# A two-layer convolution and pooling trunk: one address phase for all operands of the products, and one task for the feed-forward modulation

## The chip, the cores and the metric

The kernel runs on one core of one Trainium2 chip. The metric is the device time of one execution in microseconds (us); of several executions the median is given. A profile is one further execution, recorded instruction by instruction, with a time of its own.

The engines are named as in the profile: PE (TensorE, the products), PEld (its weight loads), DVE (VectorE), ACT (ScalarE), POOL (GpSimd), SP (SyncE, which only issues transfers). In the trace the instructions of an engine stand in the order in which the program holds them.

## The reference

The input is one sequence of 1024 positions with 1024 channels, and one conditioning vector `c`. There are two layers. In each, a modulated RMS norm feeds a token mixer (layer 0: a causal convolution module, layer 1: a causal pooling mixer), a second modulated norm feeds a gated feed-forward part, and both results are added back with a gate:

```python
c_act = jax.nn.silu(c)
for i in range(DEPTH):
    mod = c_act @ ada_w[i] + ada_b[i]
    sh_m, sc_m, g_m, sh_f, sc_f, g_f = jnp.split(mod, N_ADA, axis=-1)
    h = modulate(rms_norm(x, norm_mix_g[i]), sh_m, sc_m)
    y = conformer_conv(h, ...) if i % N_MIXERS == 0 else multiscale_pool(h, ...)
    x = x + (1.0 + g_m)[:, None, :] * y
    h = modulate(rms_norm(x, norm_ffn_g[i]), sh_f, sc_f)
    y = swiglu_ffn(h, ...)          # (silu(h @ w_gate) * (h @ w_up)) @ w_down, inner width 2816
    x = x + (1.0 + g_f)[:, None, :] * y
return rms_norm(x, final_g)
```

`conformer_conv` is a product 1024 to 2048 with a gated linear unit, a causal depthwise convolution of width 31, a layer norm over channels, silu, and a product 1024 to 1024. Everything is float32.

## The kernel before

**Layout.** Channels lie on the 128 partitions in 8 tiles (`KT`), positions along the free dimension in two chunks of 512, A and B. A chunk passes through a whole stage before the other does: the convolution part of A, then of B, and the feed-forward part of A and of B, in both layers.

**Products.** To keep float32 accuracy, both factors are split into a high and a low part. `products` (L423) issues three matmuls for each weight block of 128 x 128: weight-high by activation-high, weight-high by activation-low, weight-low by activation-high. The activations are the moving operands, 512 columns of 4 bytes; their pairs are called `hhi`/`hlo` (normed input), `vhi`/`vlo` (convolution output), `ghi`/`glo` (inside the feed-forward part), `mxhi`/`mxlo` (pooling) and `uhi`/`ulo` (the part of the depthwise convolution that is done on PE with diagonal weights). The results go to `first`, `a`, `g` (first product of the convolution module), `y` (its last product), `gate`, `up` and `dn` (feed-forward).

**Tiles of the activations.** `slot` (L239) takes one of 16 buffers for each chunk. Chunk B's are 512 floats wide. Chunk A's are 514 floats wide (`slot_after`, L243), with two columns ahead for the shifted reads of the taps on PE, and A's operands begin at the third float. `wslot` (L247) gives tiles of 542 floats (512 and a halo of 30 ahead), 8 for each chunk; `u` (convolution input), `hp` (pooling input) and `ghi`/`glo` share them. In the built program the allocator rounds the pitch of these tiles up to a multiple of 32 or 64 bytes, so the moving operands begin at these addresses modulo 256 bytes: chunk B's `hhi`, `hlo`, `vhi`, `vlo` all at 64; chunk A's at 8, 40, 72, 104, 136, 168, 200 or 232, from tile to tile; `ghi`, `glo` of both chunks at 64 or 192. All weights begin at 64.

**Taps.** The depthwise convolution of each channel tile is a `Taps` task (L666) of 31 taps, most of them `SCALAR_TENSOR_TENSOR` on DVE (`ca`), some on POOL (`pa`). For A's tile 7 all 31 taps, and for tile 6 eight of them, are done on PE (`pe_taps`, L636). `split_u` (L628) makes `uhi`/`ulo` of tile 6, `conv_glu` (L583) those of tile 7.

**Modulation.** `c_act @ ada_w` is done as dots on DVE: for 128 outputs a tile `adaw` of 128 x 1024 floats (512 KB) is loaded, multiplied by `cact` and summed (`ada_dot`, L315); 8 dots make one of the six vectors of a layer. `ada_task` (L324) does them with a pause between dots, with two buffers: a load is issued when the dot before last is done. For layer 0's feed-forward part there are two such tasks (L1144), vector 5 (gate) and vector 4 (scale), begun when the layer norm of A has been written out, ahead of A's last convolution product.

**What sets the order.** The program is written once as a list of units in PE's order. After every few products `pace` (L187) lets waiting tasks put instructions on DVE and POOL, by clocks that the planner estimates. The constants in `LOAD` are pauses of that clock. `finish` (L199) puts out all that is left of a task. Weights are loaded up to 5 ahead (`W_BUFS`): SP loads the raw tile (`raw`), ACT makes the high part and the negative of it, and a transfer of POOL's queue adds the raw tile to make the low part. SP's queue is one for `raw` and `adaw`.

**Around the change.** The order of PE there is: taps of A on PE, two tiles of B's first product, the mean of A's layer norm (`mean`), A's last product `y` in 8 output tiles with the sum of squares of the next norm behind each, one tile of B's first product (`a`, `g`) into which that norm is laid (`var`, then `rstd`), and then the first unit of the feed-forward part. All stand on DVE in the program's order with the dots.

Of the kernel before, what the change touches and what calls it, by code (L numbers as in the profile page):

```python
# [9 lines left out]
F32 = mybir.dt.float32  # L10
# [6 lines left out]
P = 128  # L17
# [9 lines left out]
PHALO = max(WINDOWS) - 1  # L27
EPS = 1e-6
# [20 lines left out]
LOAD = {"load": 4.0, "slow": 18.0, "next": 4.0, "dots": 3.5}  # L49
# [65 lines left out]
def trunk(ctx, tc, xT, c, vec, ada, adan, w1f, w1, wdg, w2, wgu, wdn, wpl, out):  # L115
# [208 lines left out]
    def ada_task(l, js, pause=None):  # L324

        def gen():
            todo = [(j, k) for j in js for k in range(KT)]
            ws = [ada_load(ada[(l * 6 + j) * KT + k]) for j, k in todo[:ADA_BUFS]]
            for i, (j, k) in enumerate(todo):
                yield pause or ("next" if lax[0] else "slow")  # L330
# [244 lines left out]
    def conv_u(ch, p):  # L575
        u = st["u", ch.i, p] = wslot(ch, "u")
# [6 lines left out]
    def conv_glu(ch, p, ba, bg):  # L583
# [3 lines left out]
        if ch.i == 0 and PE_TAPS.get(p) == CW:  # L587

            V_.scalar_tensor_tensor(ba, ba, V("conv_b1", p), sg, op0=ADD, op1=MUL)
            hi, lo = st["us", p] = [slot_after(A, name) for name in ("uhi", "ulo")]  # L590
            for part in (hi, lo):
                G_.memset(part[:, :2].bitcast(F32), 0.0)
            S_.copy(hi[:, 2:], ba)
            V_.tensor_tensor(lo[:, 2:], ba, hi[:, 2:].bitcast(F32), op=SUB)
# [6 lines left out]
    def conv_in(*todo):  # L601

        def emit(take):
            got = {}
            for each in todo:
# [30 lines left out]
    def pe_taps(p):  # L636

        groups = tap_groups(p)
        us = []
        for i, js in enumerate(groups):  # L640
            def emit(take, i=i, js=js):
# [18 lines left out]
    class Taps:  # L660
# [599 lines left out]
```

## Time and profile before

| | |
|---|---|
| runs | 1871.35, 1873.54, 1875.83 us; median 1873.54 |
| profiled execution | 1871.14 us, of which the span from first to last instruction is 1869.4 us |
| busy share of the span | PE 98%, PEld 79%, DVE 53%, ACT 52%, POOL 33% |
| mean granted clock of PE | 0.993 |
| transfers | 387.56 MB, 207 GB/s over the span |
| chain that ended last | PE 82%, DVE 10%, DMA 6%, the rest 2% |

A busy PE is not a PE at its peak: matmuls overlap, and the mean duration of one (393 ns for 512 columns) is longer than the distance from one start to the next. That distance has to be read from the starts, in the timeline of PE. Rows of the timeline give the start in us from the span's start, the time until the end of the last of the merged instructions in us, and in square brackets how long the engine stood idle before, and what ended that.

### The profile page before, as it was taken

Reading aid. Unit: us, or ns where it says so; the run is one execution under the profiler, and the core shown is the slowest. Engines: PE = TensorE matmul, PEld = TensorE weight load, DVE = VectorE, ACT = ScalarE, POOL = GpSimd, SP = SyncE. Lnnn points to the kernel's source line nnn. Section 1 sums busy time; section 2 is a strip of 40 time slices with the busy share of each in tenths; the row PEclk is TensorE's granted clock in tenths of the full one; section 3 lists DMA queues with packets and bytes.
Section 4 is the critical chain, followed back from the end, with each engine's and each line's share of the span. In section 5 each row is a group of like instructions: output and inputs, shape, how many; then the busy total and the mean of one; then the engine's idle time right before and its main releaser. Section 6 shows DMA issues by size and latency. Waiting matters only on the chain.

```text
span 1869.4 us, 21783 instructions
## 1 busy us (share of the span) xinstructions
PE 1826.0 (98%) x8085; PEld 1481.9 (79%) x8085; DVE 990.9 (53%) x1528; ACT 968.0 (52%) x1240; POOL 614.8 (33%) x662
## 2 busy tenths in 40 slices
PE   7999998999999999999999999999999999999997
PEld 5777776888888888877888888888888888888886
DVE  8899856988875235585622233734432233322225
ACT  3775665766656454454644445644534454444443
POOL 4587522877733211272111111511111111111111
PEclk9999998999999999999999999999999999999998
DMA  7958797888978987999887878778778879788782
GB/s 289 300 151 221 172 263 222 225 222 208 223 189 216 231 221 185 283 261 269 227 194 178 211 171 205 182 173 205 181 178 196 192 177 250 176 205 197 181 195 68
DMA packets 108285, 387.56 MB, mean 207 GB/s; under 512 B 11793, under 2 KB 13969, under 8 KB 108178
## 3 DMA queue, kind: packets, MB, share of 16 engines
q0 software_dynamic: 44208, 160.98, 47.2%
q1 hardware_dynamic: 62880, 224.13, 34.6%
q8 instruction: 64, 1.05, 0.2%
q10 hardware_dynamic: 1090, 1.05, 0.2%
q14 instruction: 43, 0.35, 0.1%
HBM read 381.92 MB, written 4.19 MB: 207 GB/s over the span
## 4 chain that ended last, share of the span: by engine, by line
PE 82%; DVE 10%; DMA 6%; issue 1%; ACT 1%; SPq 0%; POOL 0%; DVEq 0%
PE gate L131 24%; PE up L131 24%; PE dn L131 24%; DMA adaw<-in_ada_dram 5%; DVE ca L109 4%; PE y L131 4%; PE first L131 3%; DVE adaw L109 1%; DVE acc L109 1%; PE g L131 1%; PE a L131 1%; DVE x L109 1%; DVE t L109 1%; DMA adaw<-in_adan_dram 1%; DVE hlo L109 1%
## 5 line engine op out<-in xcount | busy, mean ns | idle before, releaser
L109 ACT CAST w<-raw 128x1024 fp32r<-128x1024 f32 x317 | 331.0, 1044 | 508.2 <-issue 303.8
L131 PE MATMUL gate<-hhi,w 128*128 128x512 f32 x1408 | 455.4, 393 | 2.3 <-DVE x L109 1.7
L131 PE MATMUL up<-hhi,w 128*128 128x512 f32 x1408 | 455.9, 393 | 0.0
L131 PE MATMUL dn<-ghi,w 128*128 128x512 f32 (+1 forms) x1440 | 445.7, 386 | 1.2 <-DMA w<-in_wdn_dram 1.2
L417 POOL DMA_DIRECT2D w<-in_wgu_dram x176 | 154.6, 878 | 779.0 <-ACT w L109 759.4
L109 ACT ACTIVATE w<-raw 128x1024 fp32r<-128x1024 f32 x307 | 323.9, 1055 | 0.0
L109 DVE SCALAR_TENSOR_TENSOR x<-dn,gains,x 128x512 f32<-128x512 f32 (+1 forms) x360 | 261.8, 735 | 115.8 <-PE dn L131 115.3
L109 DVE TENSOR_TENSOR t<-t,up 128x512 f32<-128x512 f32 x86 | 59.0, 686 | 495.0 <-PE up L131 474.8
L131 PEld LDWEIGHTS dn<-ghi,w 128*128 128x128 f32 x1440 | 267.9, 188 | 59.8 <-DMA w<-in_wdn_dram 1.6
L131 PEld LDWEIGHTS gate<-hhi,w 128*128 128x128 f32 x1408 | 264.8, 188 | 62.6 <-DVE x L109 2.5
L131 PEld LDWEIGHTS up<-hhi,w 128*128 128x128 f32 x1408 | 264.7, 188 | 59.2 <-DMA w<-in_wgu_dram 0.3
L131 PE MATMUL dn<-glo,w 128*128 128x512 f32 (+1 forms) x720 | 278.7, 387 | 0.0
L131 PE MATMUL gate<-hlo,w 128*128 128x512 f32 x704 | 276.7, 393 | 1.5 <-DVE hlo L109 1.5
L131 PE MATMUL up<-hlo,w 128*128 128x512 f32 x704 | 276.5, 393 | 0.0
L109 POOL TENSOR_TENSOR pa<-pa,pr 128x512 f32<-128x512 f32 x156 | 222.9, 1545 | 13.6 <-ACT pr L109 10.9
L109 DVE SCALAR_TENSOR_TENSOR ca<-u,vecs,ca 128x512 f32<-128x512 f32 x257 | 177.8, 745 | 0.5
L131 PEld LDWEIGHTS gate<-hlo,w 128*128 128x128 f32 x704 | 132.6, 188 | 31.5 <-DVE hlo L109 2.3
L131 PEld LDWEIGHTS dn<-glo,w 128*128 128x128 f32 x720 | 135.2, 188 | 28.1 <-issue 0.2
L131 PEld LDWEIGHTS up<-hlo,w 128*128 128x128 f32 x704 | 132.6, 188 | 29.2
L417 POOL DMA_DIRECT2D w<-in_wdn_dram x88 | 78.3, 890 | 228.4 <-ACT w L109 226.5
L109 DVE SCALAR_TENSOR_TENSOR adaw<-adaw,cact 128x1024 f32<-128x1024 f32 x80 | 118.9, 1488 | 65.1 <-DMA adaw<-in_ada_dram 65.0
L109 ACT ACTIVATE t<-gate 128x512 f32<-128x512 f32 x86 | 51.1, 594 | 157.4 <-PE gate L131 155.4
(145 smaller groups left out, 1776.7 us busy)
## 6 DMA issues: line engine op xcount, KB each, us to landing
raw<-in_wgu_dram SPq DMA_DIRECT2D x176, 512.0 KB, 7.5
w<-in_wgu_dram POOLq DMA_DIRECT2D x176, 512.0 KB, 8.1
raw<-in_wdn_dram SPq DMA_DIRECT2D x88, 512.0 KB, 5.3
w<-in_wdn_dram POOLq DMA_DIRECT2D x88, 512.0 KB, 9.4
adaw<-in_ada_dram SPq DMA_DIRECT2D x64, 512.0 KB, 7.6
raw<-in_w_dram SPq DMA_DIRECT2D x36, 512.0 KB, 6.4
w<-in_w_dram POOLq DMA_DIRECT2D x34, 512.0 KB, 8.5
adaw<-in_ada_dram SPq DMA_DIRECT2D x8, 1024.0 KB, 5.3
```

Of the source, the lines that this page charges most:

```text
L109: self.last = self.order(getattr(self.eng, name)(out, *args, **kw))
L131: last_mm[0] = nc.tensor.matmul(out, lhsT, rhs, start=start, stop=stop).ins.name
L417: order(nc.gpsimd.dma_start(low if len(src.shape) == 2 else low.rearrange("p (a b) -> p a b", a=src.shape[1]), src, accum_op=ADD))
```

## The change

Three things are changed.

**Addresses.** Chunk A's slots lose their two extra columns. The wide slots become pairs: one tile of 2 x 544 floats holds `u` (or `hp`) of two neighbouring channel tiles, or `ghi` at the front of the first half and `glo` at the end of the second (`gslots`); 4 pairs stand in for 8 singles. In the built program every moving operand of a product begins at 64 modulo 256 bytes, as the weights do, except the 93 taps of tile 7, which read shifted (at 52, 56, 180 and 184).

**Taps on PE.** Tile 6 has its eight taps on PE at even distances (j = 28, 26, ... 14), read from an unshifted copy, where it had the last eight; DVE and POOL do the other 23, the last of them in the task's end. Its split is made after A's last tile. The split of tile 7 lies in a pair of B's, with the halo columns cleared ahead of it.

**Modulation.** The two tasks of vectors 5 and 4 become one (`ada_f`), vector 4 first, whose first two loads are issued two tiles of B's first product earlier. Its first dot has the pause "slow" (18), the others "dots" (4.0, before 3.5). Behind A's last product only vector 4 is forced (`scale_done`); the rest runs on into the feed-forward part and is finished there after three units, and the task of layer 1 begins only then.

```diff
@@ tiles
     def slot(ch, name, dt=F32R):
-        return slot_after(ch, name, dt)[:, 2 - 2 * ch.i :]
-
-    def slot_after(ch, name, dt=F32R):
-        return slots.tile([P, ch.n + 2 - 2 * ch.i], dt, tag=f"s{ch.i}", name=nm(name))
-
-    def wslot(ch, name, dt=F32):
-        return slots.tile([P, ch.width], dt, tag=f"u{ch.i}", name=nm(name), bufs=KT)
+        return slots.tile([P, ch.n], dt, tag=f"s{ch.i}", name=nm(name))
+
+    def wpair(ch, name, dt=F32):
+        return slots.tile([P, 2, WSLOT], dt, tag=f"u{ch.i}", name=nm(name), bufs=KT // 2)
+
+    def wslot(ch, name, p):
+        if st.get((name, "pair", ch.i), (None,))[0] != p // 2:
+            st[name, "pair", ch.i] = p // 2, wpair(ch, name)
+        return st[name, "pair", ch.i][1][:, p % 2, : ch.width]
+
+    def gslots(ch):
+        pair = wpair(ch, "g", F32R)
+        return pair[:, 0, : ch.n], pair[:, 1, WSLOT - ch.n :]
...
@@ ffn_p1
-            hi, lo = st["g", ch.i, f] = [wslot(ch, name, F32R)[:, : ch.n] for name in ("ghi", "glo")]
+            hi, lo = st["g", ch.i, f] = gslots(ch)
...
@@ tap_groups
-    todo = list(range(CW - 1, CW - 1 - PE_TAPS[p], -1))
+    n = PE_TAPS[p]
+    todo = list(range(CW - 1, -1, -1) if n == CW else range(CW - 3, CW - 3 - 2 * n, -2))
...
@@ Taps, end of the task
             d = u[:, HALO : HALO + n]
+            if self.part is not None:
+                V_.tensor_tensor(self.acc, self.part, self.acc, op=ADD)
+            V_.scalar_tensor_tensor(d, d, w(CW - 1), self.acc, op0=MUL, op1=ADD)
             if self.awaits:
-                if self.part is not None:
-                    V_.tensor_tensor(d, self.part, self.acc, op=ADD)
-                else:
-                    S_.copy(d, self.acc)
                 V_.tensor_tensor(d, d, self.other, op=ADD)
-            else:
-                if self.part is not None:
-                    V_.tensor_tensor(self.acc, self.part, self.acc, op=ADD)
-                V_.scalar_tensor_tensor(d, d, w(CW - 1), self.acc, op0=MUL, op1=ADD)
...
@@ the order of the units
     unit(lambda take: finish(*(T["taps", 0, p] for p in range(KT) if PE_TAPS.get(p, 0) < CW)))
+
+    unit(lambda take: T.__setitem__("ada_f", ada_task(0, (4, 5), "dots", "slow")))
     for p in rest[len(rest) - HOLD - HOLD_LN : len(rest) - HOLD]:
         conv_in((B, p))
     need("ln_a")
-
-    unit(lambda take: [T.__setitem__(("ada", 0, j), ada_task(0, (j,), "dots")) for j in (5, 4)])
     sq_a = Squares(A)
     conv_out(A, sq_a, lambda take: [now(columns_done(*g)) for g in held_back])
-    unit(lambda take: finish(T["ada", 0, 4]))
+    def scale_done(take):
+        forced[0] = True
+        while (0, 4) not in ada_done:
+            step(T["ada_f"], "V")
+        forced[0] = False
+    unit(scale_done)
...
-    unit(lambda take: T.__setitem__(("ada", 1), ada_task(1, range(6))))
     taps(B, *range(KT))
     put("ln_b", lambda: layer_norm_silu(B))
     fa = ffn(A, 0, False)
     for i, (e, ws) in enumerate(fa):
+        if i == GROUP + 1:
+            unit(lambda take: finish(T["ada_f"]))
+            unit(lambda take: T.__setitem__(("ada", 1), ada_task(1, range(6))))
```

PE's own order stays nearly as it was: apart from the taps, three short groups (a `mean`, a `var` and an `rstd`, of B's norms in layer 0) move by 6 to 24 products. What moves is on DVE and SP. In the rows a name's number is its buffer; all compute rows have the line of the recording helper, L109 before and L113 after.

DVE, from the last tile but one of `y` to the norm ahead of the feed-forward part of A (`x`: the residual update, `acc`: the sum of squares, `var` and `col`: its mean and reciprocal root, `t` and `hlo`: the normed input). Before, without rows of `var` and `col` that only repeat the chain:

```order
L109 SCALAR_TENSOR_TENSOR x_3_80<-t_2438,gains,x_3_80 128x512
L109 TENSOR_TENSOR acc_2221<-acc_2221,t_2441 128x512
L109 SCALAR_TENSOR_TENSOR adaw_2325,mod<-adaw_2325,cact 128x1024
L109 SCALAR_TENSOR_TENSOR x_3_80<-t_2477,gains,x_3_80 128x512
L109 SCALAR_TENSOR_TENSOR adaw_2365,mod<-adaw_2365,cact 128x1024
L109 TENSOR_TENSOR acc_2221<-acc_2221,t_2480 128x512
L109 SCALAR_TENSOR_TENSOR adaw_2368,mod<-adaw_2368,cact 128x1024
L109 TENSOR_SCALAR var_2540<-var_2540 128x4
L109 SCALAR_TENSOR_TENSOR adaw_2408,mod<-adaw_2408,cact 128x1024
L109 SCALAR_TENSOR_TENSOR col_2546<-var_2540,col_2546 128x4
L109 SCALAR_TENSOR_TENSOR adaw_2411,mod<-adaw_2411,cact 128x1024
L109 SCALAR_TENSOR_TENSOR t_2575<-x_0_77,gains,rstd_2570 128x512
```

And after the change:

```order
L113 SCALAR_TENSOR_TENSOR x_3_80<-t_2406,gains,x_3_80 128x512
L113 SCALAR_TENSOR_TENSOR adaw_2379,mod<-adaw_2379,cact 128x1024
L113 TENSOR_TENSOR acc_2201<-acc_2201,t_2409 128x512
L113 SCALAR_TENSOR_TENSOR x_3_80<-t_2446,gains,x_3_80 128x512
L113 TENSOR_TENSOR acc_2201<-acc_2201,t_2449 128x512
L113 SCALAR_TENSOR_TENSOR adaw_2419,mod<-adaw_2419,cact 128x1024
L113 TENSOR_SCALAR var_2507<-var_2507 128x4
L113 SCALAR_TENSOR_TENSOR col_2513<-var_2507,col_2513 128x4
L113 SCALAR_TENSOR_TENSOR t_2545<-x_0_77,gains,rstd_2540 128x512
```

Of the 16 dots 14 stood ahead of `var` and 2 between it and `t`; now 9 stand ahead of `var`, none between it and `t`, and 7 stand behind in the feed-forward part, from the last rows of the norm (`hlo`) up to the first `dn` update.

SP, from the last weights of `y` and B's tile on into those of the feed-forward part (`raw<-in_w`: a weight tile of the convolution module, `in_wgu`: of gate and up, `adaw<-in_ada`: a tile for a dot). Before:

```order
L411 DMA raw_2235<-in_w_dram 128x1024
L141 DMA adaw_2156<-in_ada_dram 128x1024
L141 DMA adaw_2158<-in_ada_dram 128x1024
L411 DMA raw_2272<-in_w_dram 128x1024
L141 DMA adaw_2160<-in_ada_dram 128x1024
L141 DMA adaw_2162<-in_ada_dram 128x1024
L141 DMA adaw_2183<-in_ada_dram 128x1024
L411 DMA raw_2315<-in_w_dram 128x1024
L141 DMA adaw_2186<-in_ada_dram 128x1024
L141 DMA adaw_2207<-in_ada_dram 128x1024
L411 DMA raw_2358<-in_w_dram 128x1024
```

After:

```order
L422 DMA raw_1982<-in_w_dram 128x1024
L145 DMA adaw_1889<-in_ada_dram 128x1024
L145 DMA adaw_1891<-in_ada_dram 128x1024
L422 DMA raw_1992<-in_w_dram 128x1024
L422 DMA raw_2130<-in_w_dram 128x1024
L422 DMA raw_2136<-in_w_dram 128x1024
L422 DMA raw_2209<-in_w_dram 128x1024
L422 DMA raw_2215<-in_w_dram 128x1024
L422 DMA raw_2252<-in_w_dram 128x1024
L145 DMA adaw_2151<-in_ada_dram 128x1024
L145 DMA adaw_2178<-in_ada_dram 128x1024
L422 DMA raw_2292<-in_w_dram 128x1024
```

The first two loads now stand six weight tiles ahead of where the next two are, and from there on one load stands between weight tiles where two or three stood.

DVE, the end of the taps of A's tile 6 (`pa` is POOL's share, `ca` DVE's, `tap` PE's), before:

```order
L109 SCALAR_TENSOR_TENSOR ca_1742<-u_865,vecs,ca_1742 128x512 x10
L109 TENSOR_TENSOR u_865<-pa_1740,ca_1742 128x512
L109 TENSOR_TENSOR u_865<-u_865,tap_1674 128x512
L109 TENSOR_TENSOR acc_1333<-acc_1333,u_865 128x512
L109 TENSOR_TENSOR acc_1896<-acc_1333,u_993 128x512
```

After:

```order
L113 SCALAR_TENSOR_TENSOR ca_1735<-u_862,vecs,ca_1735 128x512 x10
L113 TENSOR_TENSOR ca_1735<-pa_1733,ca_1735 128x512
L113 SCALAR_TENSOR_TENSOR u_862<-u_862,vecs,ca_1735 128x512
L113 TENSOR_TENSOR u_862<-u_862,tap_1667 128x512
L113 TENSOR_TENSOR acc_1327<-acc_1327,u_862 128x512
```

The last tap is one row more on DVE ahead of the sum that the layer norm's `mean` waits for; POOL has one product fewer.

More of the change, by code (lines that the diff above doesn't have):

```diff
@@ L48 @@
 OUT_B = 3
-LOAD = {"load": 4.0, "slow": 18.0, "next": 4.0, "dots": 3.5}
+LOAD = {"load": 4.0, "slow": 18.0, "next": 4.0, "dots": 4.0}
 ON_DVE = (1, 4)
@@ L322, in ada_load, with ada_task @@
         return w
-    def ada_task(l, js, pause=None):
+    def ada_task(l, js, pause=None, first=None):
         def gen():
@@ L329, in gen @@
             for i, (j, k) in enumerate(todo):
-                yield pause or ("next" if lax[0] else "slow")
+                yield first if first and i == 0 else pause or ("next" if lax[0] else "slow")
                 ada_dot(ws.pop(0), l, j, k)
@@ L589, in conv_glu @@
             V_.scalar_tensor_tensor(ba, ba, V("conv_b1", p), sg, op0=ADD, op1=MUL)
[L590 removed]
+            pair = wpair(B, "us", F32R)
+            hi, lo = st["us", p] = [pair[:, i, : ch.width] for i in range(2)]
             for part in (hi, lo):
[L592 to L594 removed]
+                G_.memset(part[:, HALO - 2 : HALO].bitcast(F32), 0.0)
+            S_.copy(hi[:, HALO:], ba)
+            V_.tensor_tensor(lo[:, HALO:], ba, hi[:, HALO:].bitcast(F32), op=SUB)
             S_.copy(uhalo[:, p, :], ba[:, ch.n - HALO :])
@@ L620, in emit @@
                 conv_glu(ch, p, *b)
-                if ch.i == 0 and 0 < PE_TAPS.get(p, 0) < CW:
-                    split_u(p)
                 if ch.i == 0 and PE_TAPS.get(p, 0) < CW:
-                    T["taps", 0, p] = Taps(A, p, PE_TAPS.get(p, 0))
+                    T["taps", 0, p] = Taps(A, p)
+                if ch.i == 0 and p == KT - 1:
+                    for q in PE_TAPS:
+                        if PE_TAPS[q] < CW:
+                            split_u(q)
         tiles = list(dict.fromkeys(e[1] for e in todo if e))
@@ L645, in emit @@
                 for q, j in enumerate(js):
-                    o = (CW - 1 - j) // 2 * 2
-                    i0 = 2 - (CW - 1 - j) % 2
-                    products(b[:, o:], wt, q, [v[:, i0 : i0 + A.n - o] for v in st["us", p]], j == CW - 1, j == CW - PE_TAPS[p])
+                    full = PE_TAPS[p] == CW
+                    o = (CW - 1 - j) // 2 * 2 if full else CW - 3 - j
+                    c = j + o if full else 0
+                    products(b[:, o:], wt, q, [v[:, c : c + A.n - o] for v in st["us", p]], j == groups[0][0], j == groups[-1][-1])
                     if q % 4 == 3:
@@ L660, in trunk, with __init__ @@
     class Taps:
-        def __init__(self, ch, p, others=0):
+        def __init__(self, ch, p):
             self.ch, self.p, self.done, self.urgent = ch, p, False, False
-            self.next, self.acc, self.part = 0, None, None
-            self.end, self.awaits, self.other = CW - max(others, 1), others > 0, None
+            self.acc, self.part, self.other = None, None, None
+            others = tap_groups(p) if ch.i == 0 and p in PE_TAPS else []
+            self.todo, self.awaits = [j for j in range(CW - 1) if not any(j in js for js in others)], bool(others)
             tasks.append(self)
@@ L679, in step @@
                 return False
-            if self.next < self.end:
+            if self.todo:
                 if e == "V" and self.acc is None and sum(isinstance(t, Taps) and t.acc is not None for t in tasks) >= 2:
@@ L685, in step @@
                         return False
-                    if self.next >= self.end - 2:
+                    if len(self.todo) <= 2:
                         return False
-                j = self.next
-                self.next += 1
+                j = self.todo.pop(0)
                 if e == "V":
@@ L807, in pool_h @@
     def pool_h(ch, l):
-        hp = st["hp", ch.i] = [wslot(ch, "hp") for _ in range(KT)]
+        hp = st["hp", ch.i] = [wslot(ch, "hp", k) for k in range(KT)]
         for k in range(KT):
```

9 lines of the change are left out of this document (5 added, 4 removed).

## The prediction

> **What bounds the kernel now.** First the page:
>
> ```profile
> PE 1826.0 (98%) x8085; PEld 1481.9 (79%) x8085; DVE 990.9 (53%) x1528; ACT 968.0 (52%) x1240; POOL 614.8 (33%) x662
> PE 82%; DVE 10%; DMA 6%; issue 1%; ACT 1%; SPq 0%; POOL 0%; DVEq 0%
> ```
>
> PE is busy for 98% of the span and is 82% of the chain that ended last. Two things can shorten such a kernel: PE's remaining waits, and the distance between products. The waits of PE, longest first, and one of SP's queue in 200 to 360 us:
>
> ```profile
> PE var L131 <- DVE acc L109: 11.7, 3, 5.6
> PE mean L131 <- DVE acc L109: 1.7, 1, 1.7
> ```
>
> ```profile
> SPq L141 <- DVE adaw L109: 54.0, 15, 9.0
> ```
>
> The distance is read from the timeline of PE. Layer 1, chunk A (1107 to 1130 us) and chunk B (1699 to 1710 us), the first product of each group:
>
> ```profile
> 1107.71 0.39 PE L131 MATMUL dn<-ghi,w 128*128 128x512 f32 x1
> 1118.71 0.40 PE L131 MATMUL gate<-hhi,w 128*128 128x512 f32 x1
> 1129.91 0.40 PE L131 MATMUL gate<-hhi,w 128*128 128x512 f32 x1
> ...
> 1699.10 0.39 PE L131 MATMUL gate<-hhi,w 128*128 128x512 f32 x1
> 1709.98 0.39 PE L131 MATMUL gate<-hhi,w 128*128 128x512 f32 x1
> ```
>
> From `gate` to the next `gate` there are 48 products (24 `gate`, 24 `up`). In A they take 11.20 us, 233.3 ns each; in B 10.88 us, 226.7 ns each. The same instruction on the same shape is 6.6 ns slower on chunk A. The 48 products of `dn` take 1118.71 - 1107.71 = 11.00 us, 229.2 ns each, 2.5 ns over B's `gate`. The two chunks differ in where their tiles begin: B's all at 64 modulo 256 bytes, as the weights, A's at eight other phases, `ghi`/`glo` at 64 or 192. No wait stands between these products. It is the same in both layers, with quite different work beside PE: equal stretches of 50 us of A in layer 0, of A and of B in layer 1 (busy time of PE with its count, clock, DMA share, GB/s) hold 217, 217 and 221 products, `dn` among them.
>
> ```profile
> 400.00:450.00 50.00, 50.00 (x217) 1.00 0.91 228
> 1190.00:1240.00 50.00, 50.00 (x217) 1.00 0.87 208
> 1710.00:1760.00 50.00, 50.00 (x221) 1.00 0.87 207
> ```
>
> So I take the address for the cause.
>
> The waits of PE bunch at the norm ahead of A's feed-forward part. PE there, and the same two steps in the layer norm, where nothing was late:
>
> ```profile
> 228.77 0.95 PE L131 MATMUL var<-ones,acc 128*128 128x1 f32 x8
> 229.58 0.48 PE L131 MATMUL a<-hhi,w 128*128 128x512 f32 x1
> 232.39 1.05 PE L131 MATMUL rstd<-ident,col 128*128 128x128 f32 x8
> 233.20 0.48 PE L131 MATMUL g<-hhi,w 128*128 128x512 f32 x1
> ...
> 285.96 0.39 PE L131 MATMUL a<-hhi,w 128*128 128x512 f32 x1
> 297.06 1.87 PE L131 MATMUL var<-ones,acc 128*128 128x1 f32 x8 [5.47 <-DVE acc L109]
> 305.89 1.13 PE L131 MATMUL rstd<-ident,col 128*128 128x128 f32 x8 [1.64 <-DVE col L109]
> 310.37 0.51 PE L131 MATMUL gate<-hhi,w 128*128 128x512 f32 x1 [0.59 <-ACT hhi L109]
> 312.26 0.50 PE L131 MATMUL gate<-hlo,w 128*128 128x512 f32 x1 [1.38 <-DVE hlo L109]
> 312.59 0.40 PE L131 MATMUL gate<-hhi,w 128*128 128x512 f32 x1
> ```
>
> From 285.96 to 312.59 us PE did 48 products of `a` and `g`, 2 of `gate`, and `var` and `rstd`. At 0.227 us a product and 0.81 us for each of the two small steps (229.58 - 228.77, 233.20 - 232.39) that is 11.4 + 1.6 = 13.0 us; it took 26.6. So 13.6 us were lost there, 9.1 in the four waits, the rest to a lower clock after the first:
>
> ```profile
> 180.00:200.00 20.00, 20.00 (x87) 16.29 (x87) 20.00 (x33) 10.89 (x15) 12.48 (x12) 0.96 0.67 157
> ...
> 280.00:290.00 10.00, 10.00 (x45) 8.15 (x44) 4.34 (x8) 3.10 (x4) 0.98 (x2) 1.00 1.05 307
> 290.00:300.00 10.00, 4.53 (x18) 3.71 (x18) 4.50 (x8) 5.62 (x7) 1.76 (x2) 0.71 0.93 269
> 310.00:320.00 10.00, 8.10 (x33) 6.07 (x34) 10.00 (x16) 8.73 (x13) 1.93 (x3) 1.00 0.45 125
> 330.00:340.00 10.00, 10.00 (x44) 8.06 (x43) 10.00 (x13) 10.00 (x15) 10.00 (x9) 1.00 1.00 225
> ```
>
> (Columns: stretch, length, busy time of PE, PEld, DVE, ACT and POOL with counts, granted clock, DMA share, GB/s.) DVE was late because dots stood in its queue and waited for their loads, with the DMA engines full (1.05):
>
> ```profile
> 288.26 1.23 DVE L109 SCALAR_TENSOR_TENSOR adaw<-adaw,cact 128x1024 f32<-128x1024 f32 x1 [3.23 <-DMA adaw<-in_ada_dram]
> 293.36 1.22 DVE L109 SCALAR_TENSOR_TENSOR adaw<-adaw,cact 128x1024 f32<-128x1024 f32 x1 [1.81 <-DMA adaw<-in_ada_dram]
> 296.31 0.69 DVE L109 TENSOR_TENSOR acc<-acc,t 128x512 f32<-128x512 f32 x1
> 307.67 1.23 DVE L109 SCALAR_TENSOR_TENSOR adaw<-adaw,cact 128x1024 f32<-128x1024 f32 x1 [1.93 <-DMA adaw<-in_ada_dram]
> 308.82 2.72 DVE L109 SCALAR_TENSOR_TENSOR t<-x,gains,rstd 128x512 f32<-128x512 f32 x4
> ```
>
> **The change part by part.** *Addresses, chunk A.* The counts, from the groups of the page (three products to a weight block, two of them with the high part):
>
> ```profile
> L131 PE MATMUL gate<-hhi,w 128*128 128x512 f32 x1408 | 455.4, 393 | 2.3 <-DVE x L109 1.7 <-ACT hhi L109 0.6
> L131 PE MATMUL dn<-ghi,w 128*128 128x512 f32 x1376 | 434.1, 391 | 1.2 <-DMA w<-in_wdn_dram 1.2
> L131 PE MATMUL y<-vhi,w 128*128 128x512 f32 x256 | 80.4, 394 | 0.2 <-ACT vhi L109 0.2
> L109 DVE SCALAR_TENSOR_TENSOR ca<-u,vecs,ca 128x512 f32<-128x512 f32 x257 | 177.8, 745 | 0.5
> ```
>
> `gate` has 1408 x 1.5 = 2112 products, `up` as many, half of them A's: 2112. `y` has 384, A's half 192. Together 2304, at 6.6 ns: **-15.2 us**. The change gives A the phase that B has now, so B's rows are the price, not a guess. *Addresses, `dn`*: 1376 x 1.5 = 2064 products of both chunks at 2.5 ns: **-5.2 us**. The bounds of both are nothing (if something else slows A) and these sums.
>
> What PE gains ahead of the layer norm I count at nothing. A's first products (384, 2.5 us) come before `mean`, which waited 1.7 us for DVE; and DVE was full ahead of it (20.00 of 20 us at 180 to 200), so a faster PE only waits longer.
>
> A page speaks against this part. The Trainium skill, "TensorE: Matmul & The Clock Gate", section "Back-to-back issue gap", gives the distance for a matmul by itself as N / 2.4 + 2.5 ns, some 216 ns at N = 512, with no term for an address. By it both address terms are zero. The rows above (233.3, 229.2, 226.7) do not agree with it.
>
> *Taps.* On PE the same 24 products; on DVE one `SCALAR_TENSOR_TENSOR` more ahead of `mean`, 0.745 us by the group `ca`, in a stretch where PE waits for DVE: **+0.7 us**.
>
> *Modulation.* Nine of 16 dots are left ahead of `var`, and the loads of seven (3.7 MB, 13 us at some 290 GB/s, as at 280 to 300 us) go out of the stretch in which the DMA engines were full. One dot stands between two tiles of `y`, 24 products or 5.4 us apart, and its load was issued two dots earlier, so I expect no wait for it. Then the last sum comes about 3 us after the last `y` product (bias, update, square and sum, four steps of about the sum's 0.69 us), inside the 5.4 us that the 24 products of `a` cover. Between `rstd` and `t` no dot is left, so `t` starts 1.8 us sooner after `rstd`. What stays: `gate` reaches `hlo` after 12 products of `g` (2.7 us), and DVE needs 3.4 us from `t` to the first `hlo` (308.82 to 312.26), about 1 us; the last `hlo` has a dot and four other rows ahead of it, about 1.3 us; for a late dot 0.8. So 3.1 of 13.6 us stay: **-10.5 us**, between 0 (still late) and -13.6.
>
> The seven dots go to the start of the feed-forward part. DMA has room there at first (0.45 at 310 to 320 us) and none later (1.00). POOL is busy with B's taps, and a dot can be held up on DVE:
>
> ```profile
> 372.00 6.02 DVE L109 SCALAR_TENSOR_TENSOR adaw<-adaw,cact 128x1024 f32<-128x1024 f32 x1
> ...
> 136.65 12.78 DVE L109 TENSOR_TENSOR acc<-u,u 128x512 f32<-128x512 f32 x1
> ```
>
> At 6.02 us each they take 7 x (6.02 - 1.23) = 33.5 us of DVE more; PE needs DVE first when `dn` starts to be added to `x`, after three units, 3 x 10.9 = 32.7 us. So the cover holds even then, and nearly all behind it is B's taps, for which nothing waits until the end of A's pass. Without the cover the whole 33.5 us would show. The other way to lose is SP, where weights stand behind a dot's load that waits for its buffer: one such wait was 9.0 us, against five weights ahead (27 us). I take **+1 us**, between 0 and 9.
>
> The sum is made against the profiled execution: 1871.1 - 15.2 - 5.2 + 0.7 - 10.5 + 1.0 = 1841.9 us. The median of the runs lay 2.4 us above that execution, so I predict **1844 us**, 29 less.
>
> **The rivals.** *Only the addresses pay.* The dots that are left are late all the same, or what the norm gains, the start of the feed-forward part gives back. For it: DMA was full there, and the dots run in the same queue. Against it: nine loads where 16 were. 1873.5 - 20.4 + 0.7 + 1 = 1855 us.
>
> *Addresses don't matter.* A is slower for another reason, or the diff leaves operands where they were. Against it: the built program has all at 64 but for 93 taps, and A is slow in both layers. Only norm and taps count: 1873.5 - 10.5 + 1.7 = 1865 us. It is the case in which the page's formula would hold.
>
> *Better still.* The layer norm's sum, which was held up for 12.78 us, gets through sooner, `mean` stops waiting and nothing of the norm's 13.6 us stays: 1873.5 - 20.4 - 13.6 - 1.7 - 2.5 = 1835 us.
>
> *Slower: the moved dots are starved behind POOL.* Place: DVE from 310 to 345 us. Price: 7 x (d - 1.23) us of DVE, less 32.7 of cover. It eats the gain of 29 us and 4 more from d = 10.6 us on; at 12.78 us, the worst row, the lag is 80.9 us and the time 1844 + 48 = 1892 us. The Trainium skill, "SBUF — State Buffer", section "Who interferes with whom", says that a DVE instruction with two SBUF inputs contends with a GpSimd instruction that reads SBUF; the dots are of that kind, and the two long rows agree. Against it: one row of that length in the whole trace, and 6.02 the longest of a dot.
>
> **How the numbers follow.** The forecast, both parts paying, has 0.66, with a range of its own from 1839 to 1850 us (the norm's and the start's bounds). Only the addresses: 0.20. Addresses without effect: 0.06. Better still: 0.05. Slower: 0.03. The range 1836 to 1857 us holds the forecast and the first rival and reaches to the better case. About 0.2%, 3.7 us, is what a measurement of this kernel can tell from no change. Of the cases all but the last and a third of the third end below that: faster 0.95, same 0.02, slower 0.03.
>
> **What would show it.** In the profile after: 48 products of `gate` and `up` in A take 10.9 us (right) or 11.2 (wrong); 48 of `dn` 10.9; `var` ahead of A's feed-forward part waits under 1.5 us, and the granted clock stays at 1.00 from 290 to 310 us; `mean` waits 2 to 5 us; in the first 40 us of the feed-forward part PE waits less than 2 us in all. I would be wrong if A's distance stayed, if the first wait only moved to `rstd` or `gate`, or if PE waited for weights behind the moved loads.

## The result and the profile after

The changed kernel takes **1855.9 us** (median of 4 runs, 1852.5 to 1858.9) against 1872.4 us before (4 runs): a ratio of 0.991, interval [0.9885, 0.9935]. A second set of 6 runs gave 1855.4 us and 0.991 [0.9891, 0.9929]. The kernel became 16.5 us faster; 29 were forecast (1844 us). The time lies inside the range, at its upper end, but outside the 1839 to 1850 us that were given to the forecast itself, and at the time of the first rival (1855 us). The profiled execution took 1858.9 us with a span of 1855.6 us.

From the page after, the engines and the chain that ended last:

```profile
PE 1806.6 (97%) x8085; PEld 1481.9 (80%) x8085; DVE 987.2 (53%) x1529; ACT 972.9 (52%) x1247; POOL 622.6 (34%) x661
...
PE 77%; DVE 12%; DMA 5%; issue 1%; ACT 1%; POOL 0%; DVEq 0%; SPq 0%; ACTq 0%; POOLq 0%
```

PE is busy 19.4 us less, and its share of the chain fell from 82% to 77%: the products are closer together, and part of the time they gave up is now spent waiting. The waits of PE after (engine, what waited, for what: total us, times, longest):

```profile
PE rstd L135 <- DVE col L113: 11.6, 4, 3.4
PE var L135 <- DVE acc L113: 6.0, 2, 5.5
PE dn L135 <- DVE t L113: 4.6, 1, 4.6
PE mean L135 <- DVE acc L113: 3.9, 1, 3.9
PE gate L135 <- DVE x L113: 3.7, 2, 2.1
PE gate L135 <- DVE hlo L113: 2.7, 3, 1.8
...
PE dn L135 <- DVE x L113: 2.2, 1, 2.2
PE y L135 <- POOL vlo L113: 1.8, 1, 1.8
```

The wait of `var` ahead of A's feed-forward part is gone (the two that are left stand at the start and at the end of the program). `dn` waiting for `t` and for `x` is new. `rstd` waits no less in all than before (10.1 us): its 1.6 us at this norm are gone, and 3.1 us in layer 1 are new.

**The distance of products.** Timeline of PE after, layer 1, chunk A: the start of 48 products of `gate` and `up`, of the 48 of `dn` that follow, and of the next unit; then equal stretches of 50 us in A of layer 0, A and B of layer 1 (busy time and count of PE, PEld, DVE, ACT, POOL, granted clock, DMA share, GB/s):

```profile
1093.52 0.39 PE L135 MATMUL gate<-hhi,w 128*128 128x512 f32 x1
...
1104.39 11.04 PE L135 MATMUL dn<-g,w 128*128 128x512 f32 x48
1115.28 0.39 PE L135 MATMUL gate<-hhi,w 128*128 128x512 f32 x1
```

```profile
400.00:450.00 50.00, 50.00 (x222) 41.38 (x222) 40.06 (x54) 34.65 (x47) 40.06 (x34) 1.00 0.93 236
1190.00:1240.00 50.00, 50.00 (x223) 41.39 (x222) 27.39 (x36) 25.54 (x32) 21.58 (x20) 1.00 0.90 212
1710.00:1760.00 50.00, 50.00 (x223) 41.39 (x222) 15.13 (x21) 21.35 (x25) 7.86 (x9) 1.00 0.78 178
```

96 products in 21.76 us are 226.7 ns each; `dn` begins at 1104.39 us, so the 48 of `gate` and `up` take 10.87 us and the 48 of `dn` 10.89 us, in A as in B. 50 us hold 222 or 223 products in all three places, where they held 217, 217 and 221.

**The norm ahead of A's feed-forward part.** The same PE rows of the timeline as before the change, and the clock in the stretch:

```profile
290.53 0.95 PE L135 MATMUL var<-ones,acc 128*128 128x1 f32 x8
...
294.15 1.05 PE L135 MATMUL rstd<-ident,col 128*128 128x128 f32 x8
...
298.76 0.50 PE L135 MATMUL gate<-hlo,w 128*128 128x512 f32 x1 [0.58 <-DVE hlo L113]
...
307.54 0.50 PE L135 MATMUL gate<-hlo,w 128*128 128x512 f32 x1 [0.31 <-DVE hlo L113]
...
311.03 0.50 PE L135 MATMUL gate<-hlo,w 128*128 128x512 f32 x1 [1.82 <-DVE hlo L113]
```

```profile
290.00:300.00 10.00, 9.42 (x50) 7.71 (x49) 7.00 (x22) 5.90 (x8) 1.62 (x2) 1.00 1.03 301
```

`var` and `rstd` wait for nothing; 2.7 us of waits are left, for `hlo`; the granted clock stays at 1.00.

**The start of the feed-forward part.** Here much of the time went. First the chain of waits (start, length, what), then rows of DVE, rows of PE, and the stretch, before and after the change:

```profile
328.08 1.16 DVE adaw L113 x2
329.23 0.02 issue
329.25 13.16 DMA adaw<-in_ada_dram
342.41 0.02 issue
```

```profile
342.43 1.23 DVE L113 SCALAR_TENSOR_TENSOR adaw<-adaw,cact 128x1024 f32<-128x1024 f32 x1 [6.24 <-DMA adaw<-in_ada_dram]
343.58 0.08 DVE L113 DVE_READ_ACCUMULATOR adaw<-adaw,cact 128x1 f32 x1
343.58 1.41 DVE L113 SCALAR_TENSOR_TENSOR ca<-u,vecs,ca 128x512 f32<-128x512 f32 x2
344.90 0.68 DVE L113 TENSOR_TENSOR t<-t,up 128x512 f32<-128x512 f32 x1
```

```profile
345.64 2.93 PE L135 MATMUL dn<-g,w 128*128 128x512 f32 x6 [4.62 <-DVE t L113]
350.75 4.60 PE L135 MATMUL dn<-g,w 128*128 128x512 f32 x12 [2.18 <-DVE x L113]
```

```profile
325.00:375.00 50.00, 50.00 (x217) 40.52 (x216) 49.28 (x58) 38.75 (x52) 42.09 (x38) 1.00 0.88 222
...
325.00:375.00 50.00, 43.20 (x177) 34.76 (x176) 42.70 (x56) 31.53 (x43) 38.46 (x36) 0.90 0.86 228
```

The last dot of vector 5 is put out by `finish` ahead of the first `dn`. Its load could be issued only when the dot before last had freed a buffer (329.25), and it took 13.16 us to land, with the DMA engines full (share 1.05 from 329.25 to 342.4 us). Behind the dot in DVE's queue stands `t<-t,up` of the third unit. In the built program the products have six banks of PSUM, and the sixth output of this `dn` lies in the bank of that `up`: it could begin only when DVE had read `up`, and PE stood for 4.62 us. The seventh lies in the bank of the first, which `x` has to read, also behind the dot: 2.18 us more. The granted clock was 0.90 in the stretch, where it had been 1.00.

**Layer 1's dots.** The same happens with late dots of layer 1, at the norm of A ahead of the pooling mixer and behind it. Before the change a dot also stood in that norm's chain, behind the first `var` step and 1.27 us late (rows of DVE before, of DVE after, then of PE after):

```profile
783.70 0.17 DVE L109 TENSOR_SCALAR var<-var 128x4 f32<-128x4 f32 x1
...
785.95 2.64 DVE L109 SCALAR_TENSOR_TENSOR adaw<-adaw,cact 128x1024 f32<-128x1024 f32 x1 [1.27 <-DMA adaw<-in_ada_dram]
```

```profile
785.06 1.23 DVE L113 SCALAR_TENSOR_TENSOR adaw<-adaw,cact 128x1024 f32<-128x1024 f32 x1 [7.70 <-DMA adaw<-in_ada_dram]
786.21 0.08 DVE L113 DVE_READ_ACCUMULATOR adaw<-adaw,cact 128x1 f32 x1
786.21 0.17 DVE L113 TENSOR_SCALAR var<-var 128x4 f32<-128x4 f32 x1
...
869.77 1.85 DVE L113 SCALAR_TENSOR_TENSOR adaw<-adaw,cact 128x1024 f32<-128x1024 f32 x1 [5.79 <-DMA adaw<-in_ada_dram]
871.55 0.08 DVE L113 DVE_READ_ACCUMULATOR adaw<-adaw,cact 128x1 f32 x1
871.55 2.71 DVE L113 SCALAR_TENSOR_TENSOR x<-dn,gains,x 128x512 f32<-128x512 f32 x4
```

```profile
789.65 1.16 PE L135 MATMUL rstd<-ident,col 128*128 128x128 f32 x8 [3.10 <-DVE col L113]
...
872.34 0.50 PE L135 MATMUL gate<-hhi,w 128*128 128x512 f32 x1 [2.09 <-DVE x L113]
```

The account, in us of the profiled executions. A distance from the start of one product to the next that is over 226.7 ns (in proportion for fewer than 512 columns; the short steps `var` and `rstd`, some 0.1 us a product where nothing waits, don't count) is counted as lost: in the column "address" where it is up to 20 ns longer, else in the column of its place, waits and lower clock together.

| kernel | address, whole program | layer norm of A, 200 to 250 | norm ahead of A's feed-forward part, 275 to 325 | its start, 325 to 400 | layer 1's dots, 735 to 900 |
|---|---|---|---|---|---|
| before | 25.9 | 4.9 | 14.0 | 0.0 | 4.0 |
| the change | 2.6 | 10.1 | 3.7 | 10.2 | 12.0 |
| difference | -23.3 | +5.2 | -10.3 | +10.2 | +8.0 |

With -2.4 us ahead of 200 us these make -12.6 of the 13.8 us by which the spans differ.

### The profile page after: what moved, and what is told of

The parts are those of the page before. It is cut to its first block, busy times and chain, and to the rows that moved or that the text cites. A ratio compares the mean times of both kernels' runs of the same rounds, so it can differ in the third digit from the quotient of the medians.

```text
span 1855.6 us, 21796 instructions
## 1 busy us (share of the span) xinstructions
PE 1806.6 (97%) x8085; PEld 1481.9 (80%) x8085; DVE 987.2 (53%) x1529; ACT 972.9 (52%) x1247; POOL 622.6 (34%) x661
## 3 DMA queue, kind: packets, MB, share of 16 engines
q10 hardware_dynamic: 1090, 1.05, 0.2%
## 4 chain that ended last, share of the span: by engine, by line
PE 77%; DVE 12%; DMA 5%; issue 1%; ACT 1%; POOL 0%; DVEq 0%; SPq 0%; ACTq 0%; POOLq 0%
PE gate L135 23%; PE dn L135 23%; PE up L135 23%; PE y L135 6%; DVE ca L113 5%; DMA adaw<-in_ada_dram 4%; DVE adaw L113 2%; DVE acc L113 1%; DVE x L113 1%; DVE t L113 1%; PE a L135 1%; DVE hlo L113 1%; PE g L135 1%; DMA raw<-in_w_dram 1%; DVE u L113 1%
## 5 line engine op out<-in xcount | busy, mean ns | idle before, releaser
L113 ACT CAST w<-raw 128x1024 fp32r<-128x1024 f32 x317 | 331.2, 1045 | 486.6 <-issue 300.4
L135 PE MATMUL dn<-g,w 128*128 128x512 f32 (+1 forms) x2160 | 493.9, 387 | 7.3 <-DVE t L113 4.6
L135 PEld LDWEIGHTS dn<-g,w 128*128 128x128 f32 x2160 | 401.5, 189 | 90.9 <-DVE t L113 5.2
L135 PE MATMUL up<-hhi,w 128*128 128x512 f32 x1408 | 451.3, 390 | 0.0
L113 ACT ACTIVATE w<-raw 128x1024 fp32r<-128x1024 f32 x307 | 323.9, 1055 | 0.0
L113 DVE SCALAR_TENSOR_TENSOR x<-dn,gains,x 128x512 f32<-128x512 f32 (+1 forms) x360 | 261.0, 735 | 106.8 <-PE dn L135 103.4
L113 DVE TENSOR_TENSOR t<-t,up 128x512 f32<-128x512 f32 x86 | 59.0, 686 | 482.1 <-PE up L135 471.3
L113 POOL TENSOR_TENSOR pa<-pa,pr 128x512 f32<-128x512 f32 x163 | 235.4, 1562 | 17.8 <-ACT pr L113 15.3
L113 DVE SCALAR_TENSOR_TENSOR ca<-u,vecs,ca 128x512 f32<-128x512 f32 x249 | 173.7, 748 | 0.3
L113 DVE SCALAR_TENSOR_TENSOR adaw<-adaw,cact 128x1024 f32<-128x1024 f32 x80 | 115.0, 1439 | 64.7 <-DMA adaw<-in_ada_dram 64.7
L113 ACT ACTIVATE t<-gate 128x512 f32<-128x512 f32 x86 | 51.2, 595 | 156.7 <-PE gate L135 154.9
L113 ACT ACTIVATE pr<-u,vecs 128x512 f32<-128x512 f32 x163 | 110.0, 714 | 38.5 <-DVE u L113 16.2
L113 DVE TENSOR_TENSOR g<-t,g 128x512 fp32r<-128x512 f32 x70 | 62.3, 890 | 64.7 <-ACT g L113 64.7
```

The source lines that it names most:

```text
L113: self.last = self.order(getattr(self.eng, name)(out, *args, **kw))
L135: last_mm[0] = nc.tensor.matmul(out, lhsT, rhs, start=start, stop=stop).ins.name
```

## The experiments

**1. The addresses alone.** The changed kernel with the dots of layer 0 and the start of layer 1's task put back:

```diff
-    unit(lambda take: T.__setitem__("ada_f", ada_task(0, (4, 5), "dots", "slow")))
...
+    unit(lambda take: [T.__setitem__(("ada", 0, j), ada_task(0, (j,), "dots")) for j in (5, 4)])
...
-    unit(scale_done)
+    unit(lambda take: finish(T["ada", 0, 4]))
...
+    unit(lambda take: T.__setitem__(("ada", 1), ada_task(1, range(6))))
     taps(B, *range(KT))
...
-        if i == GROUP + 1:
-            unit(lambda take: finish(T["ada_f"]))
-            unit(lambda take: T.__setitem__(("ada", 1), ada_task(1, range(6))))
```

> The change's addresses and taps, with the modulation's dots as they were before. Theory 1 (the moved dots cost as much as they gain: ahead of A's feed-forward part 12 us less, but some 10 us more at 340 to 353 us and some 8 us more at 780 to 876 us, all of it caused by the new order of the dots): the 23 us of the addresses show alone, about 1850 us, 5 to 7 us below the whole change, with the four waits of 9 us at the norm back and no waits of over 2 us at 330 to 360 and at 780 to 880 us beyond those of the kernel before. Theory 2 (the losses at 780 to 876 us come from a faster PE that needs its weights sooner while the dots' loads share the DMA engines): they show here too, about 1857 us, as the whole change.

1852.5 us, ratio 0.9889 [0.9862, 0.9916]: 18.4 us less than the kernel before on that chip, with no help from the dots. The losses at the norm are back, and larger (18.0 us against 14.0 before: a faster PE arrives sooner at the same late dots); at 325 to 400 us 0.7 us are lost, at 735 to 900 us 6.5.

**2. The dots alone.** The kernel before with the change's order of the dots, the reverse of the diff above with the pauses of the change:

> The kernel before with the new order of the dots alone, addresses and taps as before. Theory 1: the wait for var at the norm goes, and the stalls at 340 to 353 us and at 780 to 880 us appear: 1872 - 12 + 10 + 8, about 1877 us, slower than before. Theory 2: only the stall at 340 to 353 us appears, about 1870 us. The distance of A's products stays at 233 ns, dn's at 229.

1874.6 us (10 runs), ratio 1.0021 [1.0007, 1.0035]: this part by itself makes the kernel slightly slower. The waits are those of the change, though the products are as far apart as before. DVE and PE rows of this kernel:

```profile
792.17 1.22 DVE L109 SCALAR_TENSOR_TENSOR adaw<-adaw,cact 128x1024 f32<-128x1024 f32 x1 [7.20 <-DMA adaw<-in_ada_dram]
...
793.32 0.17 DVE L109 TENSOR_SCALAR var<-var 128x4 f32<-128x4 f32 x1
```

```profile
347.92 0.80 PE L131 MATMUL dn<-ghi,w 128*128 128x512 f32 x1 [2.31 <-DVE t L109]
...
353.03 0.50 PE L131 MATMUL dn<-ghi,w 128*128 128x512 f32 x1 [2.19 <-DVE x L109]
```

Lost at the account's four places: 7.7, 5.1, 6.3 and 10.9 us. So the losses of layer 1 come with the order of the dots, not with the faster PE; theory 2 falls, theory 1 stands, with smaller sizes than it gave. (The order has two parts, the one task of vectors 4 and 5 and the later start of layer 1's; no run has one without the other.)

**3 and 4. Where the address counts.** Chunk A's tiles 32 bytes longer, so that they begin at every multiple of 32; and 128 bytes put between the moving tiles and the weights:

```diff
-        return slots.tile([P, ch.n], dt, tag=f"s{ch.i}", name=nm(name))
+        return slots.tile([P, ch.n + 8 - 8 * ch.i], dt, tag=f"s{ch.i}", name=nm(name))[:, : ch.n]
```

```diff
+    pads = ctx.enter_context(tc.tile_pool(name="pads", bufs=1))
     wts = ctx.enter_context(tc.tile_pool(name="wts", bufs=W_BUFS))
...
+    nc.gpsimd.memset(pads.tile([P, 32], F32, name="pad"), 0.0)
```

> The changed kernel, with chunk A's tiles for products 32 bytes longer, so that they begin at 64, 96, 128, ... 32 modulo 256 bytes in turn; B's tiles, g and the weights stay at 64. If the distance depends on where the moving operand stands against the weights modulo 256, A's products take 230 to 235 ns at all phases but 64, as before (about +15 us on the whole, 1871 us). If a boundary of 64 bytes is enough, those at 64, 128, 192 and 0 take 227 ns and those at 32, 96, 160 and 224 more. If a step of 32 bytes is enough (the tiles before stood at 8 modulo 32), all take 227 ns.

> The changed kernel with 128 bytes put between the moving tiles and the weights: all moving operands at 64, all weights at 192 modulo 256 bytes. If weights and moving operands must be alike, each product takes 229 to 233 ns instead of 226.7, 7300 products, +17 to +46 us. If only the moving operands must be alike among themselves, all stay at 226.7 ns and the time stays near 1856 us.

One run each: 1866.1 and 1889.6 us. The same stretches of the kernel with the weights at 192:

```profile
400.00:450.00 50.00, 50.00 (x217) 40.54 (x216) 38.54 (x55) 35.73 (x48) 38.92 (x34) 1.00 0.93 232
1190.00:1240.00 50.00, 50.00 (x217) 40.53 (x216) 37.93 (x48) 30.46 (x40) 25.42 (x22) 1.00 0.71 167
1710.00:1760.00 50.00, 50.00 (x217) 40.54 (x216) 12.17 (x18) 20.82 (x24) 7.86 (x9) 1.00 0.78 177
```

217 products everywhere: now B is as slow as A was.

**5. All at 96.** The same pad, of 32 bytes, ahead of all tiles for products:

> The changed kernel with 32 bytes put ahead of all tiles for products: moving operands and weights all at 96 modulo 256 bytes instead of 64. If the two need only be alike, the distance stays 226.7 ns and the time near 1856 us. If 64 modulo 256 is special, or a boundary of 64 bytes, products take some 232 ns as with the weights at 192 (1890 us).

1853.6 us, and the distance of the change:

```profile
1190.00:1240.00 50.00, 50.00 (x222) 41.42 (x221) 27.72 (x35) 23.62 (x30) 17.70 (x17) 1.00 0.88 209
1710.00:1760.00 50.00, 50.00 (x222) 41.42 (x221) 12.63 (x18) 21.80 (x25) 7.84 (x9) 1.00 0.79 183
```

Mean distance from one product to the next, by the addresses of its operands modulo 256 bytes in the built programs (512 columns, distances under 260 ns):

| kernel | weights | moving operand | ns (count) |
|---|---|---|---|
| before | 64 | 64 | 227.1 (3725) |
| before | 64 | 192 | 231.7 (1002) |
| before | 64 | A's eight phases, 8 + 32 k | 232.0 to 237.1 (2688) |
| the change | 64 | 64 | 226.8 (7391) |
| A in steps of 32 | 64 | 64 | 227.3 (5063) |
| A in steps of 32 | 64 | 0, 32, 96, 128, 160, 192, 224 | 231.7 to 233.0 (2347) |
| weights moved | 192 | 64 | 232.4 (7399) |
| all moved | 96 | 96 | 226.8 (7398) |

What counts in these runs is that the moving operand and the weights begin alike modulo 256 bytes. No boundary of 32, 64 or 128 bytes helps, and none is needed: at 96 and 96 a product is as fast as at 64 and 64. Why the eight phases before the change differ among themselves (232.0 to 237.1 ns) was not followed.

**6. The late dot at 345 us.** The changed kernel without vector 5 of layer 0:

```diff
-                ada_dot(ws.pop(0), l, j, k)
-                if i + ADA_BUFS < len(todo):
+                if (l, j) == (0, 5):
+                    if k == 0:
+                        G_.memset(mod[:, 5 * KT : 6 * KT], 0.0)
+                else:
+                    ada_dot(ws.pop(0), l, j, k)
+                if i + ADA_BUFS < len([t for t in todo if (l, t[0]) != (0, 5)]):
```

> The changed kernel without the eight dots and loads of modulation vector 5 in layer 0 (its columns are set to zero instead, so the gate of the first feed-forward part has another value). Theory (the stall at 340 to 353 us is the last of these dots, forced ahead of a unit's product with up while its load is late): the two waits of PE there, 4.6 and 2.2 us, and the lower clock after them go, 8 to 10 us less than the changed kernel at that point; the stalls at 780 to 876 us stay within their spread. Rival (DVE is late there because of B's taps, which share the port with POOL): the waits stay at over half.

1846.3 us. DVE is as full as it was (49.97 of 50 us, nearly all B's taps, with POOL at work), and PE loses nothing at 340 to 353 us (of the 2.6 us lost at 325 to 400 us, 2.3 are a wait of `gate` for `x` at 377.93 us):

```profile
325.00:375.00 50.00, 50.00 (x223) 41.39 (x222) 49.97 (x64) 37.80 (x52) 42.63 (x39) 1.00 0.90 224
735.00:895.00 160.00, 154.23 (x670) 125.97 (x669) 103.82 (x160) 81.03 (x104) 63.74 (x89) 0.98 0.96 271
```

The rival falls. 10.5 us are still lost at 735 to 900 us, so the two losses are separate.

**7. The first dot sooner.** One pause of the change is cut, from 18 to 6 us of products:

```diff
-LOAD = {"load": 4.0, "slow": 18.0, "next": 4.0, "dots": 4.0}
+LOAD = {"first": 6.0, "load": 4.0, "slow": 18.0, "next": 4.0, "dots": 4.0}
...
-    unit(lambda take: T.__setitem__("ada_f", ada_task(0, (4, 5), "dots", "slow")))
+    unit(lambda take: T.__setitem__("ada_f", ada_task(0, (4, 5), "dots", "first")))
```

> The changed kernel with one edit: the first dot of vectors 4 and 5 after 6 us of products instead of 18, layer 1's pace as in the change. Theory: the stalls at 340 to 353 us go and nothing else, 8 to 10 us: about 1847 us, and those at 780 to 876 us stay. Rival (a stall that goes at 345 us only shifts what waits for the DMA engines): the stalls behind it grow and less than 4 us is gained.

1845.0 us, ratio 0.9868 [0.9855, 0.9881]. Nothing is lost at 325 to 400 us, 9.0 us at 735 to 900, and the wait of `y` for `vlo` is 1.78 us as in the change.

**8 to 10. Layer 1's dots sooner.** Every 12 us of products instead of every 18 during A's feed-forward part, in the change, in the addresses alone, and in the change with the first dot after 6 us:

```diff
-                yield first if first and i == 0 else pause or ("next" if lax[0] else "slow")
+                yield first if first and i == 0 else pause or ("next" if lax[0] else "mid")
...
+LOAD = {"mid": 12.0, "load": 4.0, "slow": 18.0, "next": 4.0, "dots": 4.0}
```

The addresses alone keep `"dots": 3.5`; the third kernel has `"slow": 6.0`, which only the first dot of vectors 4 and 5 still reads.

> The changed kernel, with the dots of layer 1 every 12 us of products instead of every 18 us during layer 0's feed-forward part of A, so that some 10 fewer of the 48 are left for the stretch from 735 to 895 us. Theory (the stalls at 780 to 876 us come from dots that stand in DVE's queue waiting for loads, because so many are left there that the DMA engines are full): the 12 us of stalls there fall to 2 to 5 us, about 1848 us; the stall at 340 to 353 us stays. Rival (the stalls there are weights that come late, with a faster PE): no change there, 1856 us, or more, since the loads are spread over a stretch in which the engines are 85 to 88% busy.

> The addresses alone (dots of layer 0 as before the change), with layer 1's dots every 12 us of products. Theory: of the 6.3 us of stalls at 825 to 850 us in the addresses alone 3 to 5 go, about 1848 us; the 18 us of stalls at 275 to 325 us stay.

> The changed kernel with two edits: layer 1's dots every 12 us of products, and the first dot of vectors 4 and 5 after 6 us of products instead of 18, so that two more dots stand ahead of the norm, five instead of seven are left behind it, and none is forced ahead of a unit's product. Theory: the stall at 340 to 353 us goes (8 to 10 us), that at 780 to 876 us shrinks to 2 to 5 us, the wait for var stays under 1.5 us: about 1840 us, the time that was forecast for the change. Rival (the two dots that come sooner delay the layer norm's last rows on DVE, and y waits for vlo longer than its 1.8 us): 3 to 6 us of it are lost again, 1844 to 1846 us.

1847.3 us (0.9869 [0.9835, 0.9902]), 1853.0 us (0.9903 [0.9864, 0.9942]) and **1840.0 us (0.9827 [0.9799, 0.9854])**. The last beats both kernels: 31 us less than the one before. Its stretches, and the second of them in the change:

```profile
325.00:375.00 50.00, 50.00 (x222) 41.42 (x221) 48.67 (x63) 34.61 (x48) 39.27 (x36) 1.00 0.93 246
735.00:895.00 160.00, 158.03 (x706) 130.29 (x706) 101.42 (x159) 83.52 (x107) 62.72 (x87) 1.00 0.94 254
...
735.00:895.00 160.00, 152.70 (x663) 124.62 (x662) 100.61 (x158) 79.72 (x102) 63.89 (x89) 0.98 0.96 273
```

PE does 706 products at 735 to 895 us where the change did 663. 19 or 20 of layer 1's 48 dots start after 735 us instead of 28 or 29. On the addresses alone 2.3 us are lost there in the profile, against 6.5 and 3.3 in the two profiles at the old pace, and the medians did not fall (1852.5 and 1853.0): with runs of one kernel up to 11 us apart, 4 us can't be told here. The loss at the start in the change at this pace was 7.2 us, a little below what the change itself shows (8.8 to 10.2).

**11 and 12. The change and its addresses again, on one chip.**

> The change itself once more, on the same chip as the next two. Theory: it loses to its own addresses alone, since the new order of the dots costs some 4 us by itself (1874.6 against 1870.9 us): 1856 us.

> The addresses and taps alone once more. Theory: 1856 - 4 = 1852 us, 3 to 5 us under the whole change. If the first difference (1852.5 against 1855.9 us, on two chips) was chance, they come out alike within 2 us.

1855.4 us (0.991 [0.9891, 0.9929]) and 1851.9 us (0.9899 [0.9884, 0.9914]). The difference is the 3.5 us that were expected, but the intervals overlap. That the dots cost time is shown on the kernel before (experiment 2), and only likely on top of the addresses.

Lost at the places, in the profiles of all kernels:

| kernel | 275 to 325 | 325 to 400 | 735 to 900 |
|---|---|---|---|
| dots as before: before; addresses alone, twice | 14.0; 18.0, 17.5 | 0.0; 0.7, 0.3 | 4.0; 6.5, 3.3 |
| dots as in the change: the change, twice; all at 96; dots alone | 3.7, 5.3; 3.7; 5.1 | 10.2, 9.5; 8.8; 6.3 | 12.0, 12.8; 9.5; 10.9 |
| the same, A in steps of 32; weights moved | 3.6; 3.5 | 9.4; 9.2 | 8.4; 7.5 |
| without vector 5 | 2.3 | 2.6 | 10.5 |
| first dot after 6 | 5.3 | 0.0 | 9.0 |
| layer 1 every 12: the change; addresses alone | 5.3; 17.0 | 7.2; 1.8 | 1.7; 2.3 |
| both | 5.3 | 0.0 | 3.1 |

## Why the prediction came out as it did

**Addresses: right.** -20.4 us were forecast, with 0.7 us for the taps against it; the part alone, taps included, measured 18.4 and 19.0 us; the taps were not measured by themselves. In the trace the address term is 23.3 us, 3 more. Some 2 of these are products of `first`, `a` and `g` ahead of 238 us, which the sum left out, because what PE gains there ends in the wait for `mean`; that wait grew as expected (1.7 to 3.9 us). The rest is in `gate`, `up` and `y`, where A's products had been slower than the two groups that gave the price. The formula of the Trainium skill's page "TensorE: Matmul & The Clock Gate" (section "Back-to-back issue gap", for a matmul by itself, some 216 ns at N = 512) has no term for the address. By it the rival without effect would have held. The runs do not agree: they show 226.7 ns for operands that begin alike and 231.7 to 237.1 for others, and the measurement decides.

**The norm: right.** -10.5 us forecast, -10.3 measured in the profiles; the signs (no wait for `var`, clock at 1.00, about 3 us left in waits for `hlo`) came as written.

**The start of the feed-forward part: wrong.** The term was +1 us; 10.2 us were lost. The step that failed is the price of the seven dots: "At 6.02 us each they take 7 x (6.02 - 1.23) = 33.5 us of DVE more", set against 32.7 us of cover. It took POOL for what could hold a dot up, the adding of `dn` to `x` for the first thing that PE needs of DVE, and the cover for a store that lateness is taken from. In the trace PE first needed DVE at 340.9 us, 43 us behind the first `gate` (later than the 32.7), and still the cover did not help: the lateness was not spread over seven dots but came with one, whose load landed 13.16 us after its issue, and that dot was forced to stand just ahead of the two rows that free PE's banks, `t<-t,up` before `x`. Experiment 6 shows that it was vector 5 and not DVE's load: with DVE 49.97 of 50 us busy PE lost nothing there. In experiment 7, with the same dots and loads begun sooner, the last of them ran at 326.37 us, none was forced there, and nothing was lost. The working had named a late load only ahead of the norm, and there it had counted on buffers being ahead. The sign "in the first 40 us PE waits less than 2 us" failed by little (2.7 us), and the main wait came 3 us behind those 40.

**Layer 1: missing.** The change also moves the start of layer 1's task by three units, and the sum had no term for its 48 dots. In the profiles of the change 8.0 us more than before were lost there, and in the others with that order and pace (the repeat, all at 96, the dots alone, A in steps of 32, the weights moved) 3.5 to 8.8. As many dots are left for 735 to 900 us as before (28 and 29); what differs is where they stand: one now stands ahead of the norm's `var` step on DVE, with a load that is 7 to 8 us late. But of the 12.0 us only 5.0 are lost there (782 to 805 us), and 4.7 at 855 to 885 us, around the late dot at 869.77; with the weights moved, the same order lost 0.2 and 3.9 us at the two places. So no single dot is shown to be the cause: the runs show only that the losses come with the new order and go when 9 fewer dots are left. Why the order puts the dots there was not followed through the planner.

**The layer norm of A**: +5.2 us at 200 to 250 us, from `mean` (2.2 us more), `y` for `vlo` and the lower clock behind them. The addresses alone have it too (8.7 and 9.0 us lost, 10.1 in the change), as the working said of `mean`: a faster PE waits longer. But the dots alone lost 7.7 us there with the products as slow as before, so the faster PE is only a part of it, and the rest was not followed. It more than offsets the 3 us by which the address term was too small.

**The rivals.** "Only the addresses pay" had the right time and half of the cause: the start of the feed-forward part did give back what the norm gained (10.2 against 10.3 us). That it hit the time is luck in part. Its sum is 18.7 us below the 1873.5 us it starts from; the medians differ by 16.5 us and the spans of the two profiles by 13.8. It has no term for layer 1 (8 us lost) and none for the layer norm (5 us lost), and against these its address term was 3 us too small and 2.4 us were gained ahead of 200 us, which it left out too. The slower rival, dots starved behind POOL, did not happen: the longest dot that the trace has there (4.65 us at 319.86) held up nothing that PE waited for.

```profile
319.86 4.65 DVE L113 SCALAR_TENSOR_TENSOR adaw<-adaw,cact 128x1024 f32<-128x1024 f32 x1
```

The forecast of 1844 us was the time of a kernel in which the dots are in nobody's way; with two pauses changed it is 1840 us.

## What to carry to other kernels

When work that waits for a transfer is moved in an in-order queue, look at the very next rows behind each moved instruction and at what they free (here banks of PSUM), and price the latest single load there, not the mean of all. With two buffers, a load can be issued only when the dot before last has freed its buffer (here 13.16 us before it landed, with the DMA engines full), so such work should start early and at an even pace, and none of it should be forced at a point where the main engine waits. Where products of one shape run at two distances, compare the addresses of their operands modulo 256 bytes, the weights' too.

## What was not expected of the hardware

The 5 ns for a product whose operands do not begin alike are the same at 32, 64 or 128 bytes apart (231.7 to 233.0 ns at all seven other multiples of 32), so among these it is not a matter of distance. A single move of the weights by 128 bytes cost the whole program 41 us of product time; the time rose by only 31 us against the change's profiled execution (1889.6 and 1858.9), for the most part because the slower PE waited less: 27.4 us at the places of the account instead of 36.0 (one run). And a wait is paid for more than once here: behind the 4.62 us at 345 us the granted clock fell (0.90 over the 50 us), which made 6.8 us of waits into 10.2 us lost.
